# State-space phase tables emitted ahead of the latent attention of the first layer, and one-slot operands in the second

## The chip, the cores and the metric

The kernel runs on one core of a Trainium2 chip. Five engines work side by side, each in the order of its own instruction stream: PE (TensorE, matmuls), DVE (VectorE), ACT (ScalarE), POOL (GpSimd) and SP (SyncE), whose queue issues every DMA of this kernel. The metric is the device time of one execution in microseconds (us).

## The reference

Two trunk layers act on 256 tokens and 256 context tokens of width 1024; a second block (RWKV-7, a state-space branch S5, and a convolutional FFN) follows on the 256 tokens. In one trunk layer, h is the modulated norm of the stream:

```python
z = split_columns((rmsnorm(x, pre_g) * (1 + scale) + shift) @ w_in)
y_mla = mla_branch(z, zc, ...)        # latent attention, 8 heads, times silu(gate)
y_pool = pool_branch(z, ...)          # windowed means
y_gla = gla_branch(z, zc, ...)        # gated linear attention, both directions
out = merge_branches(z, y_mla, y_pool, y_gla, ...)   # sigmoid gates, then w_out
x = x + gate * rmsnorm(out, post_g)   # shift, scale, gate = silu(c) @ mod_w + mod_b
```

The S5 branch needs, for each of 2048 complex states, the factors `exp(lam * dt)` raised to every offset in a block of time steps. They depend on weights alone:

```python
lam = lax.complex(a_re, a_im); dt = jnp.exp(log_step)[:, None]
a_bar = jnp.exp(lam * dt)
b_bar = ((a_bar - 1.0) / lam)[..., None] * lax.complex(b_re, b_im)
_, states = lax.associative_scan(s5_combine, (a_elems, bu), axis=1)
```

## The kernel before

Activations lie transposed, features on the 128 partitions and 512 token columns (256 of context, 256 of the sequence). Every fp32 operand is held as a high and a low part, and each product is three matmuls (`mm3`, L432). Weights come in units of 1 MB as two 512 KB DMAs on SP's queue (`unit`, L404) into `raw`, a ring of seven buffers; ACT casts the high part `wh` (L425), and the low part `wl` is a subtraction on DVE, every fourth one on POOL (`split`, `lo_every`, L427). The modulation chunks (`pmod`, L606) read their four raw tiles without a split.

Everything else of 128x512 lies in the Arena, 62 slots of 2 KB a partition. `S.get()` takes the slot that has been free longest, `S.put()` gives one back. Both happen when the program is emitted: a slot that is given back can be handed out by the very next line, and the tile framework then lets the first writer of the new tile wait for the last reader of the old one. A scheduler sets the order of instructions on each engine, from the order of emission and its own estimate of times.

Layer 0 runs: four first column blocks, the two query blocks (`z_q`), four attention gates, then the latent attention (`mla_chain`: keys `pkr`, `pk`, values `pv`, queries `pq`, scores `psc`) woven with the remaining modulation chunks, the GLA queries (`z_gla_q`) and values (`pgv`); the GLA chain woven with `merge(0)`, the pooling and `merge(1)`; and at last (L1225 to L1227) `merge(2)`. With that last merge `s5_prepare` (L1341) is woven: exact exponentials and angles of 128x16 on DVE, ten steps of 128x512 that reduce the angles (L1366 to L1376), two sines on ACT (L1379), three small weight tiles written to DRAM (L1421), and 16 phase tables. A table is six POOL instructions (L1433 to L1438): four products of sines and cosines of block and offset angles, a difference and a sum, into one of two table tiles with one scratch tile each; SP writes it to DRAM (`s5t`, L1440), and the second block reads it back (L1558). Then follow `pwo` (the product with `w_out`) and the entry into layer 1.

Of the kernel before, what the change touches and what calls it, by code (L numbers as in the profile page):

```python
# [11 lines left out]
F32R = mybir.dt.float32r  # L12
# [6 lines left out]
P = 128  # L19
# [8 lines left out]
FF = 2816  # L28
MLA_SCALE = 96 ** -0.5
TAU = 16.0  # L30
NSLOT = 62
MOD_AT = (0, 1, 4)
S5_EARLY = (7, 5)

# [267 lines left out]
        self.ap, self.slot, self.state = ap, slot, state  # L302


class Halves:


# [52 lines left out]
class B:  # L360
# [74 lines left out]
    def mm3(self, ps, w, xs, cols, off=0, m=P, start=True, stop=True):  # L435

        hi, lo = w
        n, last = 0, 3 * len(xs) - 1
        for k, (xh, xl) in enumerate(xs):
            a, b = hi[:, off + k * m:off + (k + 1) * m], lo[:, off + k * m:off + (k + 1) * m]  # L440
            for u, v in ((a, xh), (a, xl), (b, xh)):
                self.nc.tensor.matmul(ps, u, v[:, cols], start=start and n == 0, stop=stop and n == last)  # L442
                n += 1


# [226 lines left out]
def trunk(b, l, xs, st, A):  # L672
# [6 lines left out]
    q0 = 0 if full else 256  # L679
    NQ = 512 - q0  # L680
    v = b.vec(f"l{l}")


    ws, pss = [], []
# [30 lines left out]
    if st is None:  # L715
        h = []
        for k in range(8):
            if k in MOD_AT:
                mod_chunk(b, l, MOD_AT.index(k) + 1, True)
            h.append((S.get(F32R), S.get(F32R)))  # L720
            build_h(b, k, xs, (0, 1), gain_, shift_, pr2, *h[k])
            for w, ps in zip(ws, pss):
                b.mm3(ps, w, h[k:], ALLC, off=k * P, start=k == 0, stop=k == 7)
        S.put(*b.slot[0])
    else:
        h, st = st
        xpart = enter(b, st, xs, 1, A[:, 2:4], lambda k: [t[:, XC] for t in h[k]], gain_, shift_, (0, 1, 3, 5, 7))
        A = next(xpart)
        for w, ps in zip(ws, pss):
            b.mm3(ps[:, 0:256], w, h, slice(0, 256))  # L730
        for k in range(8):
            if k:
                next(xpart)
            for w, ps in zip(ws, pss):
                b.mm3(ps[:, XC], w, h[k:k + 1], XC, off=k * P, start=k == 0, stop=k == 7)
        for _ in xpart:
            pass
# [12 lines left out]
    def win2(name, t, cols):  # L750
        return win_pair((name, t), (name, t + 1), cols, cols)

    misc = S.get()
    nc.scalar.copy(misc, pss[0])
    zkv, skv = S.get(), S.get()
# [6 lines left out]
    nc.scalar.copy(k2[1], pss[3])  # L762
    zq, sq = [], []
    for i, ps in enumerate(win2("q", 0, QC)):
        hi, lo, s = S.get(F32R), S.get(F32R), S.get()
        nc.scalar.activation(hi[:, QC], ps[:, QC], AF.Identity, bias=b.c("zero"), scale=v("qn", i))
        nc.vector.scalar_tensor_tensor(lo[:, QC], ps[:, QC], v("qn", i), hi[:, QC], ALU.mult, ALU.subtract)
        nc.scalar.activation(s[:, QC], ps[:, QC], AF.Square)
        zq.append((hi, lo))
        sq.append(s)  # L770
    uq = b.unit_slots(("uq", l))
    ukv = b.unit_slots(("ukv", l))
# [5 lines left out]
    def mla_prep():  # L778
        rk = b.rstd(skv, P, b.pa)
        nc.vector.tensor_mul(zkv, zkv, rk)  # L780
        kvn[:] = [parts(zkv)]
        S.put(skv)
        yield
        nc.vector.tensor_add(sq[0][:, QC], sq[0][:, QC], sq[1][:, QC])
        rq = b.rstd(sq[0][:, QC], 256, b.pb)
        qtab = [S.get(), S.get()]
        for t, r_ in zip(qtab, rope):
            nc.vector.tensor_mul(t[:, QC], r_[:, QC], rq[:, :512 - q0])
        S.put(*sq)
        yield  # L790

        kt = S.get()
        nc.vector.tensor_mul(kt[0:64], misc[0:64], rope[1][0:64])
        S.put(*rope)
        ps = b.pa.tile([P, 512], F32, tag="p", name="pkr")
        nc.tensor.matmul(ps, b.c("krsel")[0:64], kt[0:64], start=True, stop=True)
        S.put(kt)
        kh = [(S.get(F32R), S.get(F32R)) for _ in range(2)]
        for (hi, lo), rows in zip(kh, (slice(64, 128), slice(0, 64))):
            b.split_act(hi[rows], lo[rows], ps[rows])  # L800
        vt = []
        wv = parts(ukv[1])
        wk.append(parts(ukv[0]))
        for t in range(4):
            ps = b.pa.tile([P, 512], F32, tag="p", name="pv")
            (kh_, kl_), (vh_, vl_) = kvn[0], wv
            for i, (u, w) in enumerate(((kh_, vh_), (kh_, vl_), (kl_, vh_))):
                nc.tensor.matmul(ps, u[:, t * P:(t + 1) * P], w, start=i == 0, stop=i == 2)
            s = S.get()
            nc.scalar.copy(s, ps)  # L810
            vt.append(s)
        S.put(*wv)
        return qtab, kh, vt
# [3 lines left out]
    def parts(t):  # L817

        hi, lo = S.get(F32R), S.get(F32R)
        b.split_act(hi, lo, t)  # L820
        S.put(t)
        return hi, lo


    def head_scores(hd, qtab, kh):
# [14 lines left out]
        if hd % 2:  # L840
            S.put(*uqs)
        if hd == 7:
            S.put(*qtab, *kvn[0], *zq[0], *zq[1], *wk[0])
        pr = {}
        for sq_ in seqs:
            nk = 512 if sq_ else 256
# [48 lines left out]
        return g  # L895

    def finish(y):
        hi, lo = S.get(F32R), S.get(F32R)
        b.split_act(hi[:, QC], lo[:, QC], y.ap)
        S.drop(y)  # L900
        return hi, lo

    ymla, mgate = [], []

# [24 lines left out]
    mg = [None] * 8  # L929

    def merge(br, ys):
        if not isinstance(ys[0], tuple):
            ys[:] = [finish(y) for y in ys]
        for j in range(0, 8, 2):
            if j % 4 == 0:
                bu = b.unit(("br", l, br, j))
            for i, ps in enumerate(win2("merge", 8 * br + j, QC)):
                jj = j + i
                th = S.cols(NQ)
                nc.scalar.activation(th.ap, ps[:, QC], AF.Tanh, scale=0.5)  # L940
                w = b.split(bu[:, (jj % 4) * 512:(jj % 4 + 1) * 512], 512)
                pb_ = b.pmm.tile([P, 512], F32, tag="p", name="pbr")
                b.mm3(pb_[:, QC], w, ys, QC)
                nc.vector.scalar_tensor_tensor(th.ap, th.ap, 1.0, pb_[:, QC], ALU.add, ALU.mult)
                if mg[jj] is None:
                    mg[jj] = th
                else:
                    nc.vector.tensor_add(mg[jj].ap, mg[jj].ap, th.ap)
                    S.drop(th)
                yield  # L950
        for t in ys:
            S.put(*t)


    ypool = []
# [43 lines left out]
    def gla_cols():  # L999
        for ps in win2("gla_q", 0, QC):  # L1000
            s = S.get()
            nc.scalar.mul(s[:, QC], ps[:, QC], 0.125)
            q2.append(s)
            yield
        gv.extend(S.get() for _ in range(4))
        for half in range(2):
            u = b.unit(("glav", l, half))
            ws = [b.split(u[:, i * 1024:(i + 1) * 1024], 1024) for i in range(2)]
            for t in range(4):
                ps = b.pmm.tile([P, 512], F32, tag="p", name="pgv")  # L1010
                n = 0
                for k in range(8):
                    wh, wl = ws[k // 4]
                    o = (k % 4) * 256
                    for x_, w_ in ((h[k][0], wh), (h[k][1], wh), (h[k][0], wl)):
                        nc.tensor.matmul(ps[:, :256], x_[:, t * P:(t + 1) * P], w_[:, o:o + 256],
                                         start=n == 0, stop=n == 23)
                        n += 1
                nc.scalar.copy(gv[t][:, half * 256:half * 256 + 256], ps[:, :256])
                if t % 2:  # L1020
                    yield

    def gla_decay():
        es = []
# [171 lines left out]
    def cat(*gens):  # L1196
        for g in gens:
            yield from g
# [22 lines left out]
        yield from c  # L1221

    weave(mla_chain(), 14, cat(mla_gates(), turns(mods(), gla_cols())), 15 if full else 11)
    weave(gla_chain(), 46, cat(merge(0, ymla), pooling(), merge(1, ypool)), 24)
    if full:  # L1225
        b.lo_every = 1 << 30
        weave(s5_prepare(b), 19, merge(2, ygla), 8)  # L1227
        b.lo_every = 4
    else:
        for _ in merge(2, ygla):  # L1230
            pass
    for t in h:
        S.put(*t)
    merged = []
    for j in range(8):
        hi, lo = S.get(F32R), S.get(F32R)
        nc.scalar.mul(hi[:, QC], mg[j].ap, 0.5)  # L1237
        nc.vector.scalar_tensor_tensor(lo[:, QC], mg[j].ap, 0.5, hi[:, QC], ALU.mult, ALU.subtract)
        merged.append((hi, lo))
        S.drop(mg[j])  # L1240


# [21 lines left out]
                take(n, ps[:, 256 * s_:256 * s_ + 256])  # L1264
    if not full:
        for t in merged:
            S.put(*t)
        return outs[0], A

    nG, nsh = b.mod[1][1], b.mod[1][0]  # L1270
    nh = [(S.get(F32R), S.get(F32R)) for _ in range(8)]
    ctx = enter(b, outs[0], xs, 0, A[:, 0:2], lambda k: [t[:, 0:256] for t in nh[k]],
                lambda k, s_: nG[:, k, s_:s_ + 1], lambda k, s_: nsh[:, k, s_:s_ + 1], (2, 4, 6))
    for w in held:
        next(ctx)
# [5 lines left out]
        pass  # L1281
    S.put(*b.slot[0])
    for t in merged:
        S.put(*t)
    return (nh, outs[1]), A


# [811 lines left out]
```

## Time and profile before

| | us |
|---|---|
| median of 3 runs | 1564.38 (1563.26 to 1565.61) |
| profiled execution | 1565.01 |
| its span | 1563.2 |
| PE busy | 1443.2 (92%) |
| DVE busy | 1113.5 (71%) |
| ACT busy | 678.0 (43%) |
| POOL busy | 493.0 (32%) |

The profile is of one execution; 1.8 us of its time lie around the span. An engine's busy time excludes waiting, and a PE that is busy all through a stretch can be held up there by nothing else. The mean granted clock of PE is 0.955 of full speed.

### The profile page before, as it was taken

Reading aid. Unit: us, or ns where it says so; the run is one execution under the profiler, and the core shown is the slowest. Engines: PE = TensorE matmul, PEld = TensorE weight load, DVE = VectorE, ACT = ScalarE, POOL = GpSimd, SP = SyncE. Lnnn points to the kernel's source line nnn. Section 1 sums busy time; section 2 is a strip of 40 time slices with the busy share of each in tenths; the row PEclk is TensorE's granted clock in tenths of the full one; section 3 lists DMA queues with packets and bytes.
Section 4 is the critical chain, followed back from the end, with each engine's and each line's share of the span. In section 5 each row is a group of like instructions: output and inputs, shape, how many; then the busy total and the mean of one; then the engine's idle time right before and its main releaser. Section 6 shows DMA issues by size and latency. Waiting matters only on the chain. (4 is left out here: it accounts for less than half of the span.)

```text
span 1563.2 us, 26753 instructions
## 1 busy us (share of the span) xinstructions
PE 1443.2 (92%) x10316; PEld 1233.7 (79%) x10316; DVE 1113.5 (71%) x2224; ACT 678.0 (43%) x1247; POOL 493.0 (32%) x503
## 2 busy tenths in 40 slices
PE   5999998999899989889988899979899999699997
PEld 1666776887788877887777889977668999699996
DVE  4565567887789655775579887768988549798843
ACT  3434445343333334354464445633431435376642
POOL 1000003354345954320034441335543102421212
PEclk8999999999999999799999899979999999799998
DMA  9634431221124254334024245734221225266550
GB/s 355 193 107 157 131 123 41 82 68 54 47 89 131 82 170 149 95 108 162 14 68 122 81 122 166 246 124 140 89 95 36 82 70 165 78 191 186 178 187 29
DMA packets 61183, 188.19 MB, mean 120 GB/s; under 512 B 7040, under 2 KB 8448, under 8 KB 61056
## 3 DMA queue, kind: packets, MB, share of 16 engines
q1 hardware_dynamic: 61056, 186.49, 37.7%
q8 instruction: 81, 1.33, 0.4%
q14 instruction: 46, 0.38, 0.1%
HBM read 180.43 MB, written 6.03 MB: 119 GB/s over the span
## 5 line engine op out<-in xcount | busy, mean ns | idle before, releaser
L425 ACT CAST wh<-raw 128x1024 fp32r<-128x1024 f32 (+1 forms) x296 | 279.2, 948 | 286.2 <-PE y L442 55.7
L427 DVE TENSOR_TENSOR wl<-raw,wh 128x1024 fp32r<-128x1024 f32 (+1 forms) x225 | 264.9, 1179 | 163.7 <-ACT wh L425 160.2
L427 POOL TENSOR_TENSOR wl<-raw,wh 128x1024 fp32r<-128x1024 f32 (+1 forms) x71 | 144.3, 2033 | 611.2 <-ACT wh L425 596.9
L442 PE MATMUL z_merge<-s,wh 128*128 128x512 f32 (+1 forms) x768 | 196.8, 346 | 4.1 <-ACT s L940 4.1
L442 PEld LDWEIGHTS z_merge<-s,wh 128*128 128x128 f32 x768 | 134.2, 196 | 20.6 <-ACT s L940 4.9
L442 PE MATMUL z_merge<-s,wl 128*128 128x512 f32 (+1 forms) x384 | 132.3, 344 | 1.2 <-DVE wl L427 1.2
L442 PE MATMUL pbr<-s,wh 128*128 128x256 f32 (+1 forms) x512 | 119.8, 325 | 0.8 <-DVE s L433 0.8
L442 PE MATMUL pup<-s,wh 128*128 128x256 f32 x656 | 118.5, 284 | 0.1
L442 PEld LDWEIGHTS pup<-s,wh 128*128 128x128 f32 x656 | 102.5, 192 | 0.2 <-ACT wh L425 0.2
L442 PE MATMUL y<-s,wh 128*128 128x256 f32 x496 | 98.1, 295 | 0.0
L442 PE MATMUL pwo<-s,wh 128*128 128x256 f32 (+1 forms) x448 | 94.3, 308 | 3.9 <-ACT s L1237 3.1
L442 PEld LDWEIGHTS pbr<-s,wh 128*128 128x128 f32 x512 | 86.4, 191 | 9.5 <-DVE s L433 1.2
L442 PE MATMUL pup<-s,wl 128*128 128x256 f32 x328 | 92.9, 283 | 0.0
L442 PEld LDWEIGHTS y<-s,wh 128*128 128x128 f32 x496 | 78.5, 193 | 7.6 <-issue 4.7
L442 PEld LDWEIGHTS z_merge<-s,wl 128*128 128x128 f32 x384 | 74.8, 195 | 10.7 <-DVE wl L427 2.6
L442 PE MATMUL pbr<-s,wl 128*128 128x256 f32 (+1 forms) x256 | 82.9, 324 | 0.0
L442 PEld LDWEIGHTS pwo<-s,wh 128*128 128x128 f32 x448 | 75.1, 199 | 7.8 <-ACT s L1237 3.8
L1122 ACT ACTIVATE s<-s 128x512 f32<-128x512 f32 (+1 forms) x64 | 32.7, 523 | 90.0 <-DVE s L1121 69.1
L442 PE MATMUL y<-s,wl 128*128 128x256 f32 x248 | 71.3, 287 | 0.0
L1099 PE MATMUL plv<-s,s 128*128 128x128 f32 x384 | 55.4, 289 | 16.1 <-POOL s L1125 4.2
L442 PE MATMUL pwo<-s,wl 128*128 128x256 f32 (+1 forms) x224 | 68.6, 306 | 1.5 <-DVE wl L427 1.5
L432 ACT CAST s<-s 128x256 fp32r<-128x256 f32 (+1 forms) x88 | 42.6, 487 | 61.4 <-DVE s L1192 18.0
(476 smaller groups left out, 3681.9 us busy)
## 6 DMA issues: line engine op xcount, KB each, us to landing
raw<-wts SPq DMA_DIRECT2D x294, 512.0 KB, 4.4
s<-wts SPq DMA_DIRECT2D x57, 256.0 KB, 5.4
s5t<-s SPq DMA_DIRECT2D x16, 256.0 KB, 2.0
s<-s5t SPq DMA_DIRECT2D x16, 256.0 KB, 3.2
s<-xc SPq DMA_DIRECT2D x8, 256.0 KB, 4.9
x<-xc SPq DMA_DIRECT2D x8, 256.0 KB, 5.0
s<-tabs SPq DMA_DIRECT2D x4, 256.0 KB, 4.5
out<-s SPq DMA_DIRECT2D x8, 128.0 KB, 1.8
```

The source lines that it names most:

```text
L425: self.nc.scalar.copy(hi[:, :n], src)
L427: self.last_lo = eng.tensor_sub(lo[:, :n], src, hi[:, :n])
L432: self.nc.scalar.copy(hi, src)
L442: self.nc.tensor.matmul(ps, u, v[:, cols], start=start and n == 0, stop=stop and n == last)
L1099: nc.tensor.matmul(ps[:, c], K_[:, j], Z[:, c], start=True, stop=True)
L1122: nc.scalar.activation(E[:, lo:], E[:, lo:], AF.Exp, scale=1.0 / TAU)
```

## The change

`s5_prepare` is emitted in layer 0 right after the query blocks have been given their PSUM tiles, before the slots of the latent attention are taken; the low parts go to DVE alone until the latent attention is emitted. `merge(2)` stands alone. The Arena has 64 slots. In layer 1, where only the 256 sequence columns are worked on, an operand's high and low halves lie in one slot (`Narrow`) where they had two, and the context slots of h are given back after the GLA values.

```diff
-NSLOT = 62
+NSLOT = 64
+class Wide:
+    def __init__(self, S):
+        self.slots = [S.get(F32R), S.get(F32R)]
+class Narrow:
+    def __init__(self, S, seqs=(1,)):
+        self.slots = [S.get(F32R) for _ in seqs]
+        self.of = dict(zip(seqs, self.slots))
...
+    if full:
+
+        for _ in s5_prepare(b):
+            pass
+        b.lo_every = 1 << 30
     misc = S.get()
     nc.scalar.copy(misc, pss[0])
...
     weave(mla_chain(), 14, cat(mla_gates(), turns(mods(), gla_cols())), 15 if full else 11)
+    b.lo_every = 4
     weave(gla_chain(), 46, cat(merge(0, ymla), pooling(), merge(1, ypool)), 24)
-    if full:
-        b.lo_every = 1 << 30
-        weave(s5_prepare(b), 19, merge(2, ygla), 8)
-        b.lo_every = 4
-    else:
-        for _ in merge(2, ygla):
-            pass
+    for _ in merge(2, ygla):
+        pass
...
-    nh = [(S.get(F32R), S.get(F32R)) for _ in range(8)]
+    nh = [Narrow(S, (0, 1)) for _ in range(8)]
```

The lines of the changed kernel stand 24 to 37 lower than the same ones before. In the pieces below a number behind a name counts tiles; `s27_85_653` is a tile in Arena slot 27.

SP's queue, in the latent attention of layer 0; the `raw` tiles are the halves of the units that follow the attention gates (the unit numbers are one higher after the change). Before:

```order
L410 DMA raw19_0_1118<-wts 128x1024
L410 DMA raw19_1_1119<-wts 128x1024
L410 DMA raw20_0_1297<-wts 128x1024
L410 DMA raw20_1_1298<-wts 128x1024
L410 DMA raw21_0_1305<-wts 128x1024
L410 DMA raw21_1_1306<-wts 128x1024
L410 DMA raw22_0_1387<-wts 128x1024
L410 DMA raw22_1_1388<-wts 128x1024
```

After:

```order
L1477 DMA s5t11_751<-s29_87_655 128x512
L433 DMA raw20_1_1389<-wts 128x1024
L1477 DMA s5t12_759<-s27_85_653 128x512
L433 DMA raw21_0_1567<-wts 128x1024
L1477 DMA s5t13_767<-s29_87_655 128x512
L433 DMA raw21_1_1568<-wts 128x1024
L1477 DMA s5t14_775<-s27_85_653 128x512
L433 DMA raw22_0_1575<-wts 128x1024
L1477 DMA s5t15_783<-s29_87_655 128x512
L433 DMA raw22_1_1576<-wts 128x1024
```

Between any two of these weight loads now stands the write of a phase table, up to the sixteenth, `s5t15`; before, the tables stood among the loads of `merge(2)`.

ACT, around the copies of the attention values `pv`, the fourth attention gate and the casts of the first head. The `waits` name the engine or DMA queue whose signal the instruction waits for. Before:

```order
L810 COPY s15_115_817<-pv_813 128x512 [waits PE_49]
L810 COPY s16_116_823<-pv_819 128x512 [waits PE_49]
L810 COPY s1_117_829<-pv_825 128x512 [waits PE_49]
L893 ACTIVATE s2_118_860<-z0_mla_gate3_835 128x512 [waits PE_49]
L432 CAST s56_106_791<-pk_863 64x512 [waits PE_49]
L432 CAST s58_108_793<-pk_863 64x512 [waits DVE_49]
L432 CAST s45_122_883<-s44_121_882 128x512 [waits DMAHW4_49,DVE_49]
```

After:

```order
L636 COPY s40_141_1218<-pmod_1201 128x512 [waits PE_49]
L1035 ACTIVATE s16_148_1317<-z0_gla_q0_1292 128x512 [waits PE_49,Activation_49]
L843 COPY s17_131_1099<-pv_1095 128x512 [waits Activation_49,Pool_49]
L926 ACTIVATE s18_132_1130<-z0_mla_gate3_1105 128x512 [waits Activation_49]
L455 CAST s27_133_1142<-s48_100_869 128x512 [waits DMAHW4_49,DMAHW5_49,DMAHW2_49,DMAHW6_49,DMAHW1_49,DMAHW0_49]
L455 CAST s30_136_1153<-s29_135_1152 128x512 [waits DVE_49]
L448 CAST wh12_1661<-raw23_0_1657 128x1024 [waits DMAHW2_49]
```

The copy of the fourth `pv` now goes into slot 17, where the sine table lay, and waits for POOL; the cast of the query weight goes into slot 27, where one of the two table tiles lay, and waits for DMAs. The weight casts behind them (`wh12`) follow in the same stream.

PE, at the same heads. Before:

```order
L442 MATMUL pq_871<-s27_83_593,s4_120_873 128x512
L606 MATMUL pmod_931<-raw15_0_932,sc_92 32x512 x2
L606 MATMUL pmod_931<-raw15_1_933,sc_92 32x512 x2
L606 MATMUL pmod_931<-raw16_0_940,sc_92 32x512
L851 MATMUL psc_888<-s56_106_791,s45_122_883 128x256
L851 MATMUL psc_888<-s57_107_792,s45_122_883 128x256
L851 MATMUL psc_899<-s56_106_791,s45_122_883 128x256
L851 MATMUL psc_899<-s57_107_792,s45_122_883 128x256
L851 MATMUL psc_888<-s56_106_791,s18_123_884 128x256
L851 MATMUL psc_899<-s56_106_791,s18_123_884 128x256
L606 MATMUL pmod_931<-raw16_0_940,sc_92 32x512
L606 MATMUL pmod_931<-raw16_1_941,sc_92 32x512 x2
```

After:

```order
L630 MATMUL pmod_1379<-raw19_0_1380,sc_92 32x512 x2
L630 MATMUL pmod_1379<-raw19_1_1381,sc_92 32x512 x2
L630 MATMUL pmod_1379<-raw20_0_1388,sc_92 32x512 x2
L630 MATMUL pmod_1379<-raw20_1_1389,sc_92 32x512 x2
L466 MATMUL z0_gla_q1_1478<-s25_25_269,wh11_1474 128x512
L466 MATMUL z0_gla_q1_1478<-s26_26_270,wh11_1474 128x512
L466 MATMUL z0_gla_q1_1478<-s25_25_269,wl11_1475 128x512
L466 MATMUL z0_gla_q1_1478<-s38_38_326,wh11_1474 128x512
L466 MATMUL z0_gla_q1_1478<-s39_39_327,wh11_1474 128x512
L466 MATMUL z0_gla_q1_1478<-s38_38_326,wl11_1475 128x512
L466 MATMUL pq_1141<-s36_94_828,s27_133_1142 128x512
L466 MATMUL pq_1141<-s37_95_829,s27_133_1142 128x512
```

The second modulation chunk, which ends in `raw20_1`, and the first quarter of the second `z_gla_q` stand ahead of the first `pq` now, where the first `pq` and `psc` stood ahead of the first `z_gla_q`.

## Rows read from the trace of the kernel before

**Rows 1.** Page, part 1: engine, busy us (share of the span), instructions.
```profile
PE 1443.2 (92%) x10316; PEld 1233.7 (79%) x10316; DVE 1113.5 (71%) x2224; ACT 678.0 (43%) x1247; POOL 493.0 (32%) x503
```

**Rows 2.** Busy time (instructions) per engine in five stretches, named by the header.
```profile
core 0: us, PE busy (x) PEld busy (x) DVE busy (x) ACT busy (x) POOL busy (x), PEclk, DMA share, GB/s
100.00:120.00 20.00, 20.00 (x94) 13.55 (x94) 10.45 (x41) 7.99 (x16) 0.00 (x0) 1.00 0.21 63
120.00:140.00 20.00, 20.00 (x104) 12.82 (x102) 12.35 (x35) 9.55 (x22) 0.00 (x0) 1.00 0.46 155
500.00:535.00 35.00, 35.00 (x156) 28.84 (x155) 27.04 (x28) 11.46 (x18) 34.02 (x38) 1.00 0.27 90
535.00:573.00 38.00, 34.86 (x152) 27.92 (x150) 14.48 (x15) 8.41 (x13) 33.82 (x46) 1.00 0.34 111
473.00:478.60 5.60, 5.60 (x28) 4.64 (x27) 5.28 (x11) 1.89 (x3) 0.00 (x0) 1.00 0.22 77
```

**Rows 3.** PE's waits, 480 to 600: in total, times, longest us.
```profile
PE z_merge L442 <- ACT s L940: 4.1, 2, 2.7
```

**Rows 4.** SyncE's queue in time order: start us, us, form, count.
```profile
548.21 9.97 SPq L1440 DMA_DIRECT2D s5t<-s  x3
558.28 0.38 SPq L410 DMA_DIRECT2D raw<-wts  x1
```

**Rows 5.** ACT in time order; in brackets the idle before and its releaser.
```profile
562.26 1.04 ACT L425 CAST wh<-raw 128x1024 fp32r<-128x1024 f32 x1 [8.24 <-DMA raw<-wts]
```

**Rows 6.** Page, part 6: count, KB each, median us from issue to landing.
```profile
raw<-wts SPq DMA_DIRECT2D x294, 512.0 KB, 4.4
...
s5t<-s SPq DMA_DIRECT2D x16, 256.0 KB, 2.0
```

**Rows 7.** POOL in time order, one table to the next.
```profile
534.65 0.61 POOL L1434 TENSOR_TENSOR s<-s 128x256 f32<-128x256 f32 x1
...
538.35 0.61 POOL L1434 TENSOR_TENSOR s<-s 128x256 f32<-128x256 f32 x1
```

**Rows 8.** DVE in time order, before the first latent-attention operands.
```profile
64.17 1.29 DVE L433 TENSOR_TENSOR s<-s,s 128x512 fp32r<-128x512 f32 x2
68.43 1.23 DVE L427 TENSOR_TENSOR wl<-raw,wh 128x1024 fp32r<-128x1024 f32 x1 [2.97 <-ACT wh L425]
...
81.30 0.16 DVE L474 TENSOR_SCALAR m<-ps_ss 128x4 f32<-128x4 f32 x1 [3.25 <-PE ps_ss L461]
```

**Rows 9.** ACT in time order around the sine.
```profile
480.74 0.72 ACT L1379 ACTIVATE s<-s,after 128x512 f32<-128x512 f32 x1
```

**Rows 10.** PE in time order, first two attention heads.
```profile
112.12 1.52 PE L442 MATMUL pq<-s,s 128*128 128x512 f32 x6
113.57 1.90 PE L606 MATMUL pmod<-raw,sc 128*32 128x512 f32 x10
115.40 0.98 PE L851 MATMUL psc<-s,s 128*128 128x256 f32 x6
116.32 1.06 PE L606 MATMUL pmod<-raw,sc 128*32 128x512 f32 x6
117.31 0.74 PE L442 MATMUL z_gla_q<-s,wh 128*128 128x512 f32 x2
...
118.34 0.95 PE L614 MATMUL pmod<-cons,s 128*128 128x2 f32 x8
```

**Rows 11.** ACT in time order, same place.
```profile
114.40 0.62 ACT L432 CAST s<-s 128x512 fp32r<-128x512 f32 x1 [0.18 <-DVE s L836]
```

**Rows 12.** DVE in time order, same place.
```profile
113.68 0.69 DVE L836 TENSOR_TENSOR s<-pq,s 128x512 f32<-128x512 f32 x1
```

**Rows 13.** Busy time and PEclk around a wake-up of PE.
```profile
1027.00:1037.00 10.00, 3.19 (x12) 2.36 (x12) 7.36 (x27) 0.37 (x1) 5.20 (x8) 0.50 0.29 85
1037.80:1043.90 6.10, 5.94 (x26) 5.65 (x27) 6.07 (x16) 1.98 (x5) 0.97 (x2) 0.50 0.00 0
1043.90:1048.00 4.10, 4.10 (x36) 4.10 (x36) 1.20 (x3) 0.80 (x2) 0.00 (x0) 1.00 0.20 64
```

More of the change, by code (lines that the diff above doesn't have):

```diff
@@ L302, in __init__, with cut @@
         self.ap, self.slot, self.state = ap, slot, state
+class Wide:
+    def __init__(self, S):
+        self.slots = [S.get(F32R), S.get(F32R)]
+    def cut(self, cols):
+        return self.slots[0][:, cols], self.slots[1][:, cols]
+class Narrow:
+    def __init__(self, S, seqs=(1,)):
+        self.slots = [S.get(F32R) for _ in seqs]
+        self.of = dict(zip(seqs, self.slots))
+    def cut(self, cols):
+        assert cols.stop - cols.start == 256 and cols.start % 256 == 0
+        t = self.of[cols.start // 256]
+        return t[:, 0:256], t[:, 256:512]
 class Halves:
@@ L438, in mm3 @@
         n, last = 0, 3 * len(xs) - 1
-        for k, (xh, xl) in enumerate(xs):
+        for k, x in enumerate(xs):
+            xh, xl = (t[:, cols] for t in x) if isinstance(x, tuple) else x.cut(cols)
             a, b = hi[:, off + k * m:off + (k + 1) * m], lo[:, off + k * m:off + (k + 1) * m]
             for u, v in ((a, xh), (a, xl), (b, xh)):
-                self.nc.tensor.matmul(ps, u, v[:, cols], start=start and n == 0, stop=stop and n == last)
+                self.nc.tensor.matmul(ps, u, v, start=start and n == 0, stop=stop and n == last)
                 n += 1
@@ L681, in trunk @@
     v = b.vec(f"l{l}")
+    operand = lambda: (Wide if full else Narrow)(S)
     ws, pss = [], []
@@ L719, in trunk @@
                 mod_chunk(b, l, MOD_AT.index(k) + 1, True)
-            h.append((S.get(F32R), S.get(F32R)))
-            build_h(b, k, xs, (0, 1), gain_, shift_, pr2, *h[k])
+            h.append(Wide(S))
+            build_h(b, k, xs, (0, 1), gain_, shift_, pr2, *h[k].slots)
             for w, ps in zip(ws, pss):
@@ L726, in trunk @@
         h, st = st
-        xpart = enter(b, st, xs, 1, A[:, 2:4], lambda k: [t[:, XC] for t in h[k]], gain_, shift_, (0, 1, 3, 5, 7))
+        xpart = enter(b, st, xs, 1, A[:, 2:4], lambda k: h[k].cut(XC), gain_, shift_, (0, 1, 3, 5, 7))
         A = next(xpart)
@@ L764, in trunk @@
     for i, ps in enumerate(win2("q", 0, QC)):
-        hi, lo, s = S.get(F32R), S.get(F32R), S.get()
-        nc.scalar.activation(hi[:, QC], ps[:, QC], AF.Identity, bias=b.c("zero"), scale=v("qn", i))
-        nc.vector.scalar_tensor_tensor(lo[:, QC], ps[:, QC], v("qn", i), hi[:, QC], ALU.mult, ALU.subtract)
+        z, s = operand(), S.get()
+        hi, lo = z.cut(QC)
+        nc.scalar.activation(hi, ps[:, QC], AF.Identity, bias=b.c("zero"), scale=v("qn", i))
+        nc.vector.scalar_tensor_tensor(lo, ps[:, QC], v("qn", i), hi, ALU.mult, ALU.subtract)
         nc.scalar.activation(s[:, QC], ps[:, QC], AF.Square)
-        zq.append((hi, lo))
+        zq.append(z)
         sq.append(s)
@@ L780, in mla_prep @@
         nc.vector.tensor_mul(zkv, zkv, rk)
-        kvn[:] = [parts(zkv)]
+        kvn[:] = [Wide(S)]
+        b.split_act(*kvn[0].slots, zkv)
+        S.put(zkv)
         S.put(skv)
@@ L805, in mla_prep @@
             ps = b.pa.tile([P, 512], F32, tag="p", name="pv")
-            (kh_, kl_), (vh_, vl_) = kvn[0], wv
+            (kh_, kl_), (vh_, vl_) = kvn[0].slots, wv
             for i, (u, w) in enumerate(((kh_, vh_), (kh_, vl_), (kl_, vh_))):
@@ L842, in head_scores @@
         if hd == 7:
-            S.put(*qtab, *kvn[0], *zq[0], *zq[1], *wk[0])
+            S.put(*qtab, *kvn[0].slots, *zq[0].slots, *zq[1].slots, *wk[0])
         pr = {}
@@ L897, in finish @@
     def finish(y):
-        hi, lo = S.get(F32R), S.get(F32R)
-        b.split_act(hi[:, QC], lo[:, QC], y.ap)
+        z = operand()
+        b.split_act(*z.cut(QC), y.ap)
         S.drop(y)
-        return hi, lo
+        return z
     ymla, mgate = [], []
@@ L931, in merge @@
     def merge(br, ys):
-        if not isinstance(ys[0], tuple):
+        if isinstance(ys[0], Col):
             ys[:] = [finish(y) for y in ys]
@@ L951, in merge @@
         for t in ys:
-            S.put(*t)
+            S.put(*t.slots)
     ypool = []
@@ L1014, in gla_cols @@
                     o = (k % 4) * 256
-                    for x_, w_ in ((h[k][0], wh), (h[k][1], wh), (h[k][0], wl)):
-                        nc.tensor.matmul(ps[:, :256], x_[:, t * P:(t + 1) * P], w_[:, o:o + 256],
+                    s0 = 256 * (t // 2)
+                    xh, xl = h[k].cut(slice(s0, s0 + 256))
+                    for x_, w_ in ((xh, wh), (xl, wh), (xh, wl)):
+                        nc.tensor.matmul(ps[:, :256], x_[:, t % 2 * P:(t % 2 + 1) * P], w_[:, o:o + 256],
                                          start=n == 0, stop=n == 23)
@@ L1021, in gla_cols @@
                     yield
+        if not full:
+            for t in h:
+                S.put(t.of.pop(0))
+                del t.slots[0]
     def gla_decay():
@@ L1223, in trunk @@
     weave(mla_chain(), 14, cat(mla_gates(), turns(mods(), gla_cols())), 15 if full else 11)
+    b.lo_every = 4
     weave(gla_chain(), 46, cat(merge(0, ymla), pooling(), merge(1, ypool)), 24)
-    if full:
-        b.lo_every = 1 << 30
-        weave(s5_prepare(b), 19, merge(2, ygla), 8)
-        b.lo_every = 4
-    else:
-        for _ in merge(2, ygla):
-            pass
+    for _ in merge(2, ygla):
+        pass
     for t in h:
-        S.put(*t)
+        S.put(*t.slots)
     merged = []
     for j in range(8):
[L1236 to L1239, printed above, removed]
+        z = operand()
+        hi, lo = z.cut(QC)
+        nc.scalar.mul(hi, mg[j].ap, 0.5)
+        nc.vector.scalar_tensor_tensor(lo, mg[j].ap, 0.5, hi, ALU.mult, ALU.subtract)
+        merged.append(z)
         S.drop(mg[j])
@@ L1266, in trunk @@
         for t in merged:
-            S.put(*t)
+            S.put(*t.slots)
         return outs[0], A
     nG, nsh = b.mod[1][1], b.mod[1][0]
-    nh = [(S.get(F32R), S.get(F32R)) for _ in range(8)]
-    ctx = enter(b, outs[0], xs, 0, A[:, 0:2], lambda k: [t[:, 0:256] for t in nh[k]],
+    nh = [Narrow(S, (0, 1)) for _ in range(8)]
+    ctx = enter(b, outs[0], xs, 0, A[:, 0:2], lambda k: nh[k].cut(slice(0, 256)),
                 lambda k, s_: nG[:, k, s_:s_ + 1], lambda k, s_: nsh[:, k, s_:s_ + 1], (2, 4, 6))
@@ L1283, in trunk @@
     for t in merged:
-        S.put(*t)
+        S.put(*t.slots)
     return (nh, outs[1]), A
```

## The prediction

> **What bounds the kernel now.** I read the page first: PE is busy 92% of the span [rows 1], so a saving on another engine shows only where PE waits. Then busy time by stretches: where the change puts the tables (100 to 140) PE is busy all the time, and where they come from (500 to 573) it idles 3.1 us in all [rows 2]. PE's waits between 480 and 600 give the price of the old place: 4.1 us for gates of the last merge [rows 3]. SP's queue shows the reason. It issues in order; a table's write waits for POOL, and a weight load behind it waits with it: three tables hold the queue from 548.21 to 558.28 [rows 4], and ACT's cast at 562.26 had been idle 8.24 us for that load [rows 5]. So in-order queues behind POOL are what to follow, and the question is what stands behind POOL in the new place.
>
> **The new place.** Two chains lead there from POOL's tables to PE. One is SP's: the load `raw20_1`, which the second modulation chunk reads, stands behind twelve tables, `raw22_1` behind all sixteen. The other is the Arena's. The tables' slots are given back when the tables are emitted, and the attention's tiles take them: ACT's copy of the fourth `pv` goes into the sine's slot and waits until POOL has read it for the last time, the cast for the first `pq` goes into a table tile and waits for the landing of table 14, and the DVE product behind that `pq` for that of table 15. Everything later on ACT and DVE stands behind these. Both chains end when POOL does. The sum needs three times: when POOL starts, when it ends, when PE would have been there.
>
> **POOL's start: about 85.** The angles are ready when DVE has gone through its stream, which ends the operand splits at 64.17 + 1.29 = 65.4 and then idled several times until 81.3 [rows 8]. Ahead of the sines the new order has four weight splits of 1.23 (4.9), three operations like the 0.69 one [rows 12] (2.1), the ten angle steps (5.3 [rows 2]) and some 35 operations of 128x16 at 0.16 [rows 8] (5.6): 17.9 us, so 83.3 if DVE no longer idles. Two sines of 0.72 [rows 9] give 84.7. I take 85, give or take 3.
>
> **POOL's rate.** With DVE almost silent, a table takes 538.35 - 534.65 = 3.70 us, 0.617 for each of its six operations [rows 7]. With DVE busy 38% of a stretch it is 33.82/46 = 0.735, with 77% 34.02/38 = 0.895 [rows 2]. In the new place DVE is busy 52 and 62%; between the two I take 0.80 while PE and DVE run, and 0.617 once they stand.
>
> **PE's arrival.** Before, the first `z_gla_q` begins at 117.31, after the first `pq` (113.57 - 112.12 = 1.45) and `psc` (116.32 - 115.40 = 0.92) [rows 10], which come behind it now; so it would begin at 114.9. Its 24 matmuls at 1.45/6 = 0.242 are 5.8, the small `pmod` beside it 0.95, and three quarters of a chunk (1.83 + 0.99 = 2.8) 2.1 [rows 10]: PE comes to `raw20_1` at 123.8. With 0.7 for the last quarter and six matmuls it would be at the first `pq` at 126.0; then 15 matmuls (3.6), six `psc` (0.9), six matmuls (1.5), three quarters of the third chunk (2.1) and six `psc` of 512 columns (1.5): at `raw22_1` at 135.6. What the added DVE work delays before that (a query split a few us later) is swallowed by the stall.
>
> **The stall.** By 123.8 POOL has done 38.8/0.80 = 48 of 96 operations; the other 48 at 0.617 take 29.6, so the tables end at 153.4. On the way table 11 (74 operations) ends at 139.8, and `raw20_1` lands 4.4 later [rows 6]: 16 us of stall that the next wait contains. The `pq` can start about when POOL ends. Then come the landing of table 15 (2.0 [rows 6]), the product of 0.69 [rows 12], the cast of 0.62 [rows 11], and some 0.7 of signals between: `psc` at 157.4. Behind it 0.9 + 1.5 + 2.1 + 1.5 = 6.0 to `raw22_1`, which PE passes at 163.4 (it has landed by then: 153.4 + 0.5 + 4.4 = 158.3). Against 135.6 that is **27.8 us lost**.
>
> **Other terms.** *Clock.* In the stretch 1027 to 1037, in which PE did 3.19 us of work, the granted clock was 0.50; it stayed so for 6.1 us after PE had resumed. In these PE did 26 matmuls, and then 36 in 4.1 at full clock [rows 13], so waking cost about 6.1 - 26 x 4.1/36 = 3.1. Here PE wakes twice, but the first time another wait follows: +3 (0 to 6). *Cover.* The second `z_gla_q` (5.8) covered the latencies of later heads and is now used up first: +2 (0 to 5.8). *The old place.* No table stands among the loads of `merge(2)`: -4.1 [rows 3]. POOL and DVE have 60 us less to do there, beside a PE that was busy: nothing. *Three splits* that POOL did go to DVE, which gets done before PE does: nothing. *Layer 1.* `Narrow` frees slots, and no PE wait that I found there was for a slot; the matmuls are the same ones: 0, within 3 either way. *Memory traffic* is unchanged in amount; three loads (the block's vectors and two weight tiles) move into the start, in a gap of SP's queue.
>
> The sum is 27.8 + 3 + 2 - 4.1 = +28.7 on the profiled execution, 1565.0: 1593.7. That execution is 0.6 above the median, so I predict **1593**.
>
> **A rule weighed.** Rows 2 and 7 show POOL slower by 0.12 an operation with DVE busy 38%, by 0.28 with 77%. The Trainium skill ("SBUF — State Buffer", section "SBUF: two separate sides") says that VectorE and GpSimd share a pair of ports as an exclusive lock: a VectorE operation with two SBUF inputs and a GpSimd operation that reads SBUF take turns, and the loser blocks fully. By that rule the trace should show much more than it does: the measured rise is a fraction of what strict turns give, so the rule goes only into a rival.
>
> **The rivals.**
> *Strict turns.* If POOL gets only the share that DVE leaves free, an operation takes 0.617/0.43 = 1.43 at 57%: 27 by 123.8, 69 left, end at 166.4, so 13 us more: 1606. Against it: at 77% it would be 2.7, and 0.895 was measured. A milder form has the same end: 0.895 until the stall and 0.735 after (43 done, 53 left, end at 162.8) gives +9.4; with the upper clock and cover terms (+6.8) 1609.
> *Quiet tables.* If POOL keeps 0.617 all the way and starts at 82, it ends at 141.2, 12.2 earlier: 1581; with neither clock nor cover 1576.
> *No hold, faster than before.* PE would lose nothing if the sine's slot were read out and the tables' landings done before it comes to the first `pq` at 126.0; then only the old place's gain is left: 1565.0 - 4.1 - 0.6 = 1560. It decides if POOL ends by about 125, so at 40/96 = 0.42 an operation; the fastest one seen is 0.617, or the start would have to be at 66. For it speaks only that the order of instructions is sure and its times are not, and that layer 1 may hide a gain that I price at nothing.
> *The change moves nothing.* It would need the tables to stay where they are; the POOL stream has all 96 operations right behind the second weight split, so they move.
>
> **Chances.** Forecast (1582 to 1603) 0.52; strict turns or slow tables (1603 to 1612) 0.16, beyond 0.05; quiet tables (1570 to 1582) 0.13; faster 0.09, and 0.05 in between, where 0.2% or 3.1 us is about what a measurement can tell from no change. Slower so has 0.86. The range 1572 to 1610 leaves out 0.14 below and some 0.06 above.
>
> **What would show it.** Right: between about 124 and 157 PE is nearly idle, released at a `pmod` by a `raw` load and at `pq` and `psc` by ACT; ACT's copy of the fourth `pv` shows a wait of some 30 us for POOL; POOL's tables run from about 85 to 153 without gaps, faster at the end; a half clock after the wake; no 4.1 us at `z_merge`; equal distances from there to the end. Wrong: POOL done before 130; PE busy through 120 to 160; or the waits as told and the time given back in later stretches, which PE's busy share leaves little room for.

## The result, and the profile after

Four runs of the changed kernel have a median of 1589.53 us (1587.13 to 1599.2), four of the kernel before beside them 1564.99 (1563.26 to 1566.27). The ratio is 1.016 (interval 1.0137 to 1.0184): the change makes the kernel slower by about 25 us, and the forecast was 1593. The profiled execution took 1588.05, its span 1586.3, against 1565.01 and 1563.2. "Offset" below is how much later the same instruction starts in the trace after than in the one before.

The first part of the page hardly shows it (it answers to [rows 1]):

```profile
PE 1447.3 (91%) x10316; PEld 1235.0 (78%) x10316; DVE 1126.0 (71%) x2223; ACT 679.3 (43%) x1247; POOL 482.9 (30%) x504
```

Busy time by stretches of the kernel after, with the instructions of each engine, the granted clock of TensorE, the DMA share and GB/s, answers to [rows 2]:

```profile
core 0: us, PE busy (x) PEld busy (x) DVE busy (x) ACT busy (x) POOL busy (x), PEclk, DMA share, GB/s
80.00:100.00 20.00, 16.40 (x66) 13.25 (x65) 20.00 (x33) 8.36 (x11) 20.00 (x23) 0.83 0.32 110
88.10:93.70 5.60, 5.60 (x16) 4.54 (x17) 5.60 (x8) 1.70 (x3) 5.60 (x7) 0.50 0.41 108
100.00:120.00 20.00, 14.61 (x45) 10.21 (x44) 12.62 (x19) 3.42 (x6) 20.00 (x30) 0.74 0.49 154
109.00:118.20 9.20, 9.20 (x21) 6.05 (x22) 3.26 (x5) 2.83 (x5) 9.20 (x16) 0.52 0.85 257
120.00:140.00 20.00, 15.69 (x82) 9.32 (x81) 13.43 (x5) 2.35 (x4) 20.00 (x33) 0.96 0.53 172
138.70:141.60 2.90, 2.90 (x7) 1.04 (x8) 2.90 (x1) 0.00 (x0) 2.90 (x6) 0.50 0.58 170
140.00:160.00 20.00, 14.69 (x57) 9.43 (x58) 14.30 (x17) 5.23 (x10) 7.73 (x13) 0.79 0.73 226
...
148.00:152.20 4.20, 4.16 (x10) 3.33 (x11) 1.31 (x3) 0.00 (x0) 0.00 (x0) 0.53 0.95 276
```

PE is not full in any of the four stretches from 80 on, where before it was full from 100 on. It gets about half the clock in four places (0.50 to 0.53), and each begins just behind an idle time of PE. POOL is full from 80 to 140. And look at DVE: 20.00 busy with 33 instructions between 80 and 100, then 13.43 with five between 120 and 140. Before, it did 35 in 12.35 in the second of these. PE's waits in the kernel after, the five longest from 80 to 260 (in total, times, longest):

```profile
PE ps_rb L493 <- DVE r L521: 9.0, 2, 5.4
PE pq L466 <- ACT s L455: 5.3, 1, 5.3
PE pmod L630 <- DMA raw<-wts: 4.3, 1, 4.3
PE psc L884 <- ACT s L889: 1.4, 1, 1.4
PE psc L884 <- ACT s L455: 1.4, 1, 1.4
```

The second and third line are the two chains of the prediction, the slots' and SP's. The first is not in it: a broadcast of a reciprocal root, whose vector DVE makes in nine tiny steps (L513 to L521). The kernel before has 2.0 us there. Next come POOL, PE, ACT and SP in time order, the rows on which the two chains are read (start, duration, instruction, count; in brackets the idle before and its releaser):

```profile
79.91 1.73 POOL L1471 TENSOR_TENSOR s<-s 128x256 f32<-128x256 f32 x2 [52.59 <-ACT s L1416]
...
146.98 0.75 POOL L1475 TENSOR_TENSOR s<-s,s 128x256 f32<-128x256 f32 x1
```

```profile
108.97 1.12 PE L493 MATMUL ps_rb<-cons,r 128*128 128x128 f32 x4 [5.39 <-DVE r L521]
...
138.70 1.92 PE L630 MATMUL pmod<-raw,sc 128*32 128x512 f32 x4 [4.32 <-DMA raw<-wts]
...
148.04 1.22 PE L466 MATMUL pq<-s,s 128*128 128x512 f32 x2 [5.31 <-ACT s L455]
```

```profile
146.40 0.59 ACT L843 COPY s<-pv 128x512 f32<-128x512 f32 x1 [13.17 <-POOL s L1472]
```

```profile
134.23 0.32 SPq L1477 DMA_DIRECT2D s5t<-s  x1
134.64 0.38 SPq L433 DMA_DIRECT2D raw<-wts  x1
```

The load of `raw20_1` stands right behind a table's write, is issued at 134.64, and PE has it at 138.70. ACT's copy into the sine's slot waits 13.17 us and starts when POOL has read the sine for the last time (L1472, in the last table). Now DVE, in four of the nine steps and later:

```profile
104.67 0.57 DVE L515 TENSOR_TENSOR t<-t,m 128x4 f32<-128x4 f32 x1
105.28 0.54 DVE L516 SCALAR_TENSOR_TENSOR r<-t,r 128x4 f32<-128x4 f32 x1
105.85 0.54 DVE L517 TENSOR_TENSOR t<-r 128x4 f32<-128x4 f32 x1
106.43 0.54 DVE L518 TENSOR_TENSOR t<-t,m 128x4 f32<-128x4 f32 x1
...
127.95 0.23 DVE L644 TENSOR_TENSOR GP<-pmod,vec_l 128x4 f32<-128x4 f32 x2 [1.21 <-PE pmod L638]
128.15 19.68 DVE L649 TENSOR_TENSOR GP<-GP,vec_l 128x4 f32<-128x4 f32 x2
147.75 0.67 DVE L927 SCALAR_TENSOR_TENSOR s<-s,z_mla_gate 128x512 f32<-128x512 f32 x1
```

The last of these four (L494 there) in the kernel before:

```profile
97.15 0.16 DVE L494 TENSOR_TENSOR t<-t,m 128x4 f32<-128x4 f32 x1
```

A step on 128 by 4 numbers takes 0.54 to 0.57 after the change, about one POOL instruction, where it took 0.16 before. At 128.15 two more of that size take 19.68, nearly all of it the first one, and POOL's last instruction ends then (146.98 + 0.75 = 147.73). The two just ahead of them, with an operand from PSUM (the matmuls' result memory), take 0.23 together. So DVE is held out while POOL's stream runs; in this stream no operation with an operand from PSUM is lengthened, the long ones have all inputs in SBUF. The profile counts the time of being held out as busy, so DVE's busy time does not exclude waiting. That is a third chain from POOL to PE.

Where the loss was made: PE comes to `raw22_1` at about 160.2, after 511 matmuls, and the kernel before had done 512 by 135.6 (partly others, as the order differs), so it is some 24.6 us late. PE was idle 36.3 us of the first 160.2 and 19.2 of the first 135.6 before, so 17.1 more; the rest, about 7.5, is PE busy for longer (123.9 against 116.4), with half clock in the stretches above. The later offsets: +25.0 at the 193rd `z_merge` (at 430), +17.7 when the first `pwo` begins, +13.9 at the start of layer 1, +22.7 at its end, +23.1 at the end.

### The profile page after: what moved, and what is told of

The parts are those of the page before. It is cut to its first block, busy times and chain, and to the rows that moved or that the text cites. A ratio compares the mean times of both kernels' runs of the same rounds, so it can differ in the third digit from the quotient of the medians.

```text
span 1586.3 us, 26727 instructions
## 1 busy us (share of the span) xinstructions
PE 1447.3 (91%) x10316; PEld 1235.0 (78%) x10316; DVE 1126.0 (71%) x2223; ACT 679.3 (43%) x1247; POOL 482.9 (30%) x504
```

## The experiments

Each was timed in three rounds beside the kernel before, and the ratio is to it. Numbers one to four shared a chip and the runs of the kernel before; so did numbers five to eight, and so did the last two.

**The move without the smaller slots.** Edit, against the kernel after (the context slots of h are not given back early either):

```diff
-    operand = lambda: (Wide if full else Narrow)(S)
+    operand = lambda: Wide(S)
...
-    nh = [Narrow(S, (0, 1)) for _ in range(8)]
+    nh = [Wide(S) for _ in range(8)]
```

> The early s5_prepare alone; layer 1 keeps its operands in two slots as before. The profile of the change shows it 13.9 us late at the start of layer 1 and 22.7 us late at its end. Theory A (the one-slot operands or what they let be prefetched cost layer 1 its 9 us): layer 1 as before, so about 1565 + 14 = 1579. Theory B (layer 1 is slower for a reason that the move brings along, such as loads that are now issued at other times): about 1589, as with the whole change.

Measured: 1605.13 (1593.09 to 1608.59), ratio 1.022 (1.017 to 1.027), slower than the whole change, which no expectation had. DVE of this kernel, and PE's longest wait:

```profile
123.32 28.66 DVE L992 TENSOR_SCALAR psh<-vec_l 128x4 f32<-128x4 f32 x1 [3.15 <-DMA vec_l<-v_l]
```

```profile
PE pmod L638 <- ACT s L636: 23.4, 1, 23.4
```

The same hold on DVE, with another victim: an operation of 128 by 4 for 28.66 us, until the tables ended at 151.96. In this order it caught another operation, some 5 us earlier: ACT's cast of a `pk` waits 24.50 us for the DVE product behind it, and the copy that PE waits for stands behind that cast. So the move carries the loss.

**The smaller slots alone.** Edit, against the kernel after: the block goes back behind the last merge.

```diff
-        for _ in s5_prepare(b):
-            pass
...
+        weave(s5_prepare(b), 19, merge(2, ygla), 8)
```

> One-slot operands in layer 1 and 64 slots, with s5_prepare back in the last merge of layer 0. Theory A: slower than before by the 9 us of layer 1, about 1573, lost between the first scores and the end of its GLA chain. Theory B, which is what the prediction said of this part (0, within 3): 1562 to 1568.

Measured: 1567.67 (1564.51 to 1573.25), ratio 1.0013 (0.9996 to 1.003), no difference that can be measured. Its profiled execution is the slowest of its ten; DVE and a wait of PE in it:

```profile
548.03 9.48 DVE L450 TENSOR_TENSOR wl<-raw,wh 128x1024 fp32r<-128x1024 f32 x1 [15.01 <-ACT wh L448]
```

```profile
PE z_merge L466 <- DVE wl L450: 8.3, 1, 8.3
```

A weight split of 1.2 us took 9.48 beside the tables: such a hold can come at the old place as well. In the trace of the kernel before, no DVE operation beside the tables lasts over 2.88.

**The tables' slots kept until PE is past them.** This cuts the chain of the slots, and leaves SP's.

```diff
-    S.put(sn, cs, *ring[0], *ring[1])
+    b.s5["hold"] = [sn, cs, *ring[0], *ring[1]]
...
+        if hd == 3 and full:
+            S.put(*b.s5.pop("hold"))
```

> The whole change, but the slots of the sines and the table tiles are given back only at the fourth attention head, so that no tile of the first heads waits for POOL. Theory A (the prediction's: two queues behind POOL, of which the slot chain ends last): the 5.3 us wait at the first pq goes, the wait at raw20_1 and one at raw22_1 stay, 4 to 10 us less: 1580 to 1586. Theory B (the loss is made earlier, by DVE beside POOL, and the slots only collect it): under 2 us less, 1587 to 1590.

Measured: 1588.41 (1588.05 to 1593.55), ratio 1.0144 (1.012 to 1.0169): nothing gained. DVE and PE's waits:

```profile
130.88 0.69 DVE L456 TENSOR_TENSOR s<-pk,s 64x512 fp32r<-64x512 f32 x1
131.61 19.10 DVE L456 TENSOR_TENSOR s<-s,s 128x512 fp32r<-128x512 f32 x1
```

```profile
PE psc L886 <- DVE s L456: 18.1, 1, 18.1
PE ps_rb L493 <- DVE r L521: 15.0, 2, 11.4
```

The first `pq` no longer waits. The DVE product behind it waits for no slot and no load, starts, and lasts 19.10 us, to POOL's end; the one ahead of it, with an operand from PSUM, takes 0.69 as `pq`'s product did before [rows 12]. Here PE's whole stall names DVE. Not all of it is the hold: within the 11.4, DVE itself waits 4.84 for the load `vec_l`, which stands behind table writes in SP's queue.

**The tables written by POOL's own queue.** This takes the writes out of SP's queue, and leaves the slots.

```diff
-        nc.sync.dma_start(d, tab)
+        nc.gpsimd.dma_start(d, tab)
```

> The whole change, but the 16 tables are written to DRAM from POOL's own queue, so that no weight load stands behind a table on SP's queue. Theory A: the 4.3 us wait at raw20_1 goes, but the first pq still waits for the table tiles, and by itself this gives back little: 1586 to 1590. Theory B (SP's queue is the whole cost): back by most of the 24 us, under 1575.

Measured: 1598.06 (1595.48 to 1603.42), ratio 1.0203 (1.0175 to 1.023): slower still. The tables now run from 81.75 to 160.1, 78 us for 68, since each write takes POOL time too. PE's waits:

```profile
PE ps_rb L493 <- DVE r L521: 18.9, 2, 11.3
PE pq L466 <- ACT s L455: 16.0, 1, 16.0
```

The wait for `raw` is gone, the slots' wait has grown, as the tables end later. One thing changed for the good: no DVE operation lasted longer than 3.83 us. The writes may break POOL's stream, but this is not shown: the same edit in the kernel before, further down, lengthens DVE's operations.

**Both together.** The edits of the last two.

> The whole change with both chains cut: the tables' slots are given back only at the fourth head, and the tables are written from POOL's queue. Theory B (the chains are the loss): PE at its first psc as before, give or take the half clock, 1566 to 1573. Theory A (POOL's stream keeps DVE out of work, whatever the chains): with the writes from POOL's queue no DVE operation was held longer than 3.8 us, but PE was already 22.7 us late at the first pk, where no chain had bound yet; so 1578 to 1588.

Measured: 1578.57 (1577.1 to 1582.01), ratio 1.0088 (1.0067 to 1.0108). PE's waits, and two stretches (columns as above):

```profile
PE ps_rb L493 <- DVE r L521: 21.2, 2, 13.6
PE py L918 <- ACT s L914: 0.9, 1, 0.9
```

```profile
100.00:120.00 20.00, 9.16 (x42) 6.78 (x40) 19.90 (x23) 3.76 (x6) 19.91 (x26) 0.77 0.55 185
...
140.00:160.00 20.00, 20.00 (x102) 14.01 (x97) 14.39 (x36) 8.24 (x21) 17.53 (x28) 1.00 0.70 232
```

Both chains are cut: neither `pmod` nor `pq` waits, and PE is full from 140 on while POOL still runs. Yet it is 14 us slower than before, and what is left is the reciprocal root, with DVE 19.90 us busy for 23 instructions. So cutting both chains brings 11 us of the 25. What is left names DVE alone; how much of it is the hold, and how much POOL's stream made longer by its writes, was not taken apart.

**The change without POOL's stream.** Only two of the 96 table operations are left, so the tables are not computed; their slots and writes are as in the kernel after.

```diff
-        nc.gpsimd.tensor_tensor(a3(tab[:, 0:256]), can, cbn, ALU.mult)
...
+        if i < 2:
+            nc.gpsimd.tensor_tensor(tab, cs, sn, ALU.mult)
```

> The whole change, slots and SP queue as in it, but of the 96 POOL operations only two are left (each table tile is filled once; the 16 writes go out as before), so the phase tables are wrong. Both theories: no DVE operation held, no wait at pq or raw20_1. What remains is the s5 work on DVE, the order of layer 1 and the gain at the last merge: 1560 to 1572. If it stays over 1580, POOL was not the cause.

Measured: 1554.5 (1551.81 to 1555.83), ratio 0.9934 (0.9913 to 0.9954). PE's waits from 40 to 260, and one step of a reciprocal root on DVE:

```profile
PE ps_rb L493 <- DVE r L521: 1.1, 1, 1.1
```

```profile
83.58 0.16 DVE L518 TENSOR_TENSOR t<-t,m 128x4 f32<-128x4 f32 x1
```

The step is back at 0.16, and all nine of the second root take 0.16 or 0.17. POOL's stream costs the change 35 us, by all three chains together; all else in the block (angles, sines, loads, writes) makes PE wait no more than 1.1 us there, and without tables at either place the kernel is 10 faster than before.

**The kernel before, tables written by POOL's queue.** The edit of the fourth experiment, in the kernel before.

> The kernel before, with the 16 tables written from POOL's own queue instead of SP's, so that no weight load of the last merge stands behind a table. If the 4.1 us of PE waiting there come from SP's queue alone: 1560 to 1562. If POOL's longer stream (some 0.65 us more a table, by the run with this queue) slows DVE as much there: 1564 to 1570.

Measured: 1575.85 (1574.08 to 1576.03), ratio 1.0065 (1.0048 to 1.0082). The expectation missed it. The stretch of [rows 2] and PE's waits from 480 to 620:

```profile
500.00:535.00 35.00, 20.36 (x84) 15.43 (x82) 31.99 (x19) 7.40 (x12) 33.93 (x52) 0.79 0.38 127
```

```profile
PE pbr L442 <- ACT s L432: 8.2, 2, 7.4
PE pbr L442 <- DVE s L433: 6.5, 2, 3.4
```

```profile
496.75 7.42 DVE L1413 TENSOR_TENSOR s<-s,s 128x512 f32<-128x512 f32 x1
```

DVE does 19 instructions in that stretch instead of 28, and PE falls from 35.00 to 20.36. Its longest operation beside the tables, the row above, takes 7.42 us, and four more take 3.6 to 4.3; before, the same one took 2.88 and was the longest. SP's queue is free of tables here, and the wait of [rows 3] is gone, but larger ones stand in its place.

**The kernel before, tables on DVE.** In this and the next two the six operations of each table go to DVE; nothing else is edited.

```diff
-        nc.gpsimd.tensor_tensor(a3(tab[:, 0:256]), can, cbn, ALU.mult)
+        nc.vector.tensor_tensor(a3(tab[:, 0:256]), can, cbn, ALU.mult)
...
```

> The kernel before, with the six operations of a table on DVE instead of POOL, still beside the last merge. DVE was busy 60 of 92 us there, part of it slowed by POOL; 96 operations of about 0.36 us add 35. If DVE outside POOL's way has room for them: 1560 to 1566. If DVE becomes the limit of that stretch: 1568 to 1580.

Measured: 1556.56 (1552.94 to 1559.83, five runs), ratio 0.9942 (0.992 to 0.9963), faster.

```profile
500.00:535.00 35.00, 35.00 (x156) 28.99 (x155) 34.29 (x82) 13.11 (x21) 0.00 (x0) 1.00 0.51 174
535.00:573.00 38.00, 38.00 (x169) 31.46 (x168) 28.18 (x51) 12.57 (x19) 0.00 (x0) 1.00 0.49 161
```

DVE does 82 instructions in the stretch in which it did 28 beside POOL, and PE is full through both (before, it idled 3.1 us in the second). A table operation takes DVE 0.41 where it took POOL 0.61 [rows 7]; one follows the next every 0.34.

**The kernel after, tables on DVE.**

> The whole change, with the six operations of a table on DVE instead of POOL; slots and SP's queue as in the change. Theory A (what costs is POOL's stream beside DVE, not the place): no DVE operation is held, DVE has some 35 us more to do where it was 50 to 60% busy, so about 1555 to 1566. Theory C (the place is wrong in itself: whatever makes the tables there, weight loads and attention tiles wait for them): 1575 to 1590.

Measured: 1579.14 (1578.57 to 1580.17, five runs), ratio 1.01 (1.0069 to 1.0131).

```profile
PE pv L841 <- DVE s L456: 7.5, 2, 6.3
PE pkr L829 <- DVE s L826: 5.9, 1, 5.9
```

```profile
100.00:120.00 20.00, 11.35 (x55) 4.77 (x48) 18.11 (x53) 1.20 (x2) 0.00 (x0) 0.74 0.84 274
120.00:140.00 20.00, 12.53 (x33) 7.97 (x34) 18.02 (x50) 5.17 (x8) 0.00 (x0) 0.57 0.42 147
```

With POOL out of it the change still loses 15 us: the tables stand ahead of the attention's own DVE work, in order, and PE waits for that.

**The smaller slots, the old place, tables on DVE.**

> One-slot operands in layer 1, s5_prepare in the last merge as before, tables on DVE. If the one-slot operands add nothing and take nothing: as the kernel before with tables on DVE, 1553 to 1560. If they cost layer 1 time by themselves: 1560 to 1568.

Measured: 1547.92 (1547.42 to 1549.64, five runs), ratio 0.9907 (0.9876 to 0.9938): faster than both kernels, and by more than expected. Its stretches:

```profile
500.00:535.00 35.00, 35.00 (x156) 28.97 (x155) 34.05 (x80) 12.02 (x18) 0.00 (x0) 1.00 0.47 156
535.00:573.00 38.00, 38.00 (x169) 31.48 (x168) 26.12 (x45) 14.74 (x20) 0.36 (x1) 1.00 0.52 167
```

They are like those of the kernel before with tables on DVE. The base is the kernel of the second experiment. It is 9 us below the kernel before with tables on DVE, from other runs and with an interval that overlaps; where the further gain comes from was not isolated, as the smaller slots alone gave nothing.

This run and the last one differ in the place alone, so the place costs 31 us with tables on DVE. With tables on POOL it costs some 23, by the ratios of the kernel after (1.016) and of the smaller slots alone (1.0013). So the new place costs PE time whichever of the two engines makes the tables: what PE needs next there is DVE's, and DVE is either held out by POOL or busy with the tables.

## Why the prediction was right, and where it was not

The sign, the size and the place held: 28.7 predicted, 23.1 between the spans and 24.5 between the medians measured, and the loss is made between 80 and 160 by POOL's tables. The way there held in part only, and that the total came so near is partly luck. Point by point:

*The two chains: right in kind, too large in size.* Both waits stand in the trace with the releasers named: `pmod` for `raw` behind a table's write, ACT's fourth copy for POOL. But that copy waits 13.17 us where some 30 were named, and PE, named as nearly idle from 124 to 157, was busy 23.38 of these 33 us. Cutting both chains gave 11 us; cutting one gave none, or a loss (with a stream 10 us longer). All three chains end with POOL, so one can stand in for another.

*POOL's start and rate.* It began at 79.91, not 85: the work ahead of the sines was done sooner than my sum had it. The tables took 67.8 us, against 153.4 - 85 = 68.4 predicted, so the stream ended at 147.73 instead of 153.4. The course is as told, too: 53 operations in the 40 us to 120 (0.75 each; 0.80 forecast), then 33 in 20 (0.61; 0.617 forecast), though PE was not yet standing then (15.69 of 20 busy), and DVE stood because it was held out.

*PE's arrival: wrong.* It came to `raw20_1` at 138.70 - 4.32 = 134.4, not at 123.8, and to the first `pq` at 142.7, not at 126.0. The working said that delayed DVE work ahead of that is swallowed by the stall. As POOL sets the end of the stall, the total came out near; but the waits that I named are 4.3 + 5.3 = 9.6 us, not some 28, and 15 of the 24.6 were lost elsewhere: 7.0 at the broadcasts (3.60 and 5.39, where the kernel before has 2.0 in all) and about 7.5 in PE being busy for longer, with the half clock.

*The rule weighed: the step that failed.* The prediction looked at how much POOL slows when DVE is busy, found little, and put turns on a lock aside as a rival. The rows that bear on it were DVE's: 28 instructions that fill 27.04 us beside POOL, against 41 in 10.45 without it [rows 2], though not of the same kinds. It is DVE that is held out. The run without POOL's stream shows it by taking the stream away (a step takes 0.16 again, the whole 35 us less), and the run with both chains cut by the waits that it leaves (21.2 us for the roots' last step on DVE). The Trainium skill ("SBUF — State Buffer", section "SBUF: two separate sides") says that whichever of the two starts first has the shared pair of ports for the whole instruction and the other blocks. DVE's side agrees (0.54 to 0.57 a step; operations with an operand from PSUM not lengthened), and goes further: 19.68 us is a hold over some thirty POOL instructions, not over one.

*The clock: a term that was mis-sized.* Three was taken, for one wake; there were four stretches at about half clock, 5.6 + 9.2 + 2.9 + 4.2 us, and PE's busy time grew by about 7.5. *Cover:* two was taken; the offset grows by 0.4 between 160 and 430. Together the sum up to there was 27.8 + 3 + 2 = 32.8, measured 25.0.

*The old place.* PE has no wait left from 480 to 620. The offset falls by 7.3 between the 193rd `z_merge` and the first `pwo` (4.1 predicted) and by 3.8 more to the start of layer 1 (nothing predicted). Of the 3.8, 1.6 is PE's waiting for ACT and DVE at `pwo`, which it no longer does; the rest was not taken apart.

*Layer 1.* 0 within 3 was predicted, and the offset grows by 8.8. In the other runs with the early block it grows by 5 to 13; in the four with the block at the old place, two of them with the smaller slots, it changes by -1.1 to +2.3. So it comes along with the move and not with the slots. In the run without the tables it is still 6.2, with the same order of instructions in layer 1 on PE, DVE, ACT and POOL as in the kernel after; so most of it is not made by POOL's stream. The orders of all four differ from those of the kernel before; which of these does it was not taken apart.

So 32.8 - 4.1 = 28.7 stands against 25.0 - 7.3 - 3.8 + 8.8 + 0.4 = 23.1: the loss up to 430 was put 7.8 us too high and the gain at the old place 7.0 too low, and a loss of 8.8 in layer 1 was left out. The last miss has the other sign and hides more than half of the first two.

Open is also why one DVE operation gets in after a single POOL instruction (from 104.67 to 109) and another is kept out for thirty. It was not tried with a gap put between POOL's instructions alone.

## What to carry to other kernels

Look at what a long POOL stream does to DVE's small operations beside it, not only at how fast POOL runs: instructions per busy microsecond of DVE, with POOL quiet and busy, tell it. When several chains end at the same event, cutting one may gain nothing, as here; cut all of them in one run, or take the event away, before judging any. Work for an idle engine belongs where the engines that it slows have time; here, at either place, it was cheaper on the busier engine.

## What the runs showed of the hardware

- A DVE operation with its inputs in SBUF can be held until a stream of POOL instructions ends: 28.66 and 19.68 us for 128 by 4, 19.10 for 128 by 512, 9.48 for 128 by 1024. In the kernel after, an operation with an operand from PSUM keeps its time beside the same stream (0.67 to 0.73 for 512 columns).
- A table operation takes DVE 0.41 us and POOL 0.61 or more. Sixteen writes of 256 KB issued by POOL made its stream some 10 us longer in the kernel after, and cost the kernel before 11.
